# Up-weights' low half in one step, four kinds of side work in half as many visits, and a new list of shifted chunks, in a one-core hybrid decoder layer

## The chip, the cores and the metric

The kernel runs on one core of one Trainium2 chip. The metric is the device time of one launch in microseconds (us). The kernel before takes 1874.46 us in the median of 3 runs (1874.23 to 1876.05).

## What is computed

One decoder layer on 256 tokens of width 2048, in float32. Three sublayers stand behind one another, each with a root-mean-square norm before and after it and a residual:

```python
def hybrid_mixer(h, ...):
    proj = h @ w_in                                    # 2048 x 10536
    mlstm_p, rwkv_p, gate_p = split_cols(proj, ...)
    hm = mlstm_chunkwise(q, k, v, ig, logf)            # 4 heads, key width 128, value width 256
    ha = sigmoid(o) * head_norm(hm)
    rp = rwkv_p + (shift_right(rwkv_p, 1) - rwkv_p) * mu
    w_log = -softplus(-(w0 + tanh(wl) @ w_up)) - 0.5   # w_up: 64 x 1024
    a = sigmoid(a0 + al @ a_up)                        # a_up: 64 x 1024
    g = sigmoid(gl) @ g_up                             # g_up: 160 x 1024
    y = rwkv7_scan(r, decay, kr, v, kk, kk * a)        # 16 heads of 64
    hb = (group_norm(y) + bonus) * g
    merged = sigmoid(g_a) * (ha @ w_branch_a) + sigmoid(g_b) * (hb @ w_branch_b)
    return merged @ w_out

x = x + rms_norm(hybrid_mixer(rms_norm(x)))
x = x + rms_norm(cross_attention(rms_norm(x), rms_norm(mem)))   # 4 heads of 128, 256 memory tokens
x = x + rms_norm(conv_glu_ffn(rms_norm(x)))                     # 2048 -> 2 x 8192 -> 2048, a causal convolution of 3 taps
```

## The kernel before

**The main stream.** All large matrices are cut into 648 pieces of 128 partitions x 1024 elements, called chunks here and numbered in the order in which TensorE (PE) uses them. SyncE loads a chunk's 512 KB into `raw`. ScalarE (ACT) rounds it to `wh` (`Feed.hi`, L376), VectorE (DVE) forms the remainder `wl = raw - wh` (`Feed.lo`, L397). Every product is then the sum of three matmuls, high x high, low x high and high x low. A chunk of a block of kind `fm` gives 24 matmuls with 256 moving columns (128 for each of two `kj` halves times 3), a chunk of kind `tm` 12 matmuls with 512. Each of `raw`, `wh` and `wl` has four buffers, so a cast of chunk i + 4 waits until the matmuls of chunk i are done.

**Blocks and evacuation.** `run` walks through the blocks (16 to 32 chunks of weights that share an accumulator). A finished block leaves a generator (`evac`) that empties its PSUM banks on DVE and ACT. The accumulators are four banks, so a block may begin only when the block two before it has been emptied.

**The side work.** Everything that isn't the main stream, such as gates, group sums, the chunked recurrences and norms, stands in Python generators. `Spread.half` is called at each half chunk (12 `fm` matmuls or 6 `tm` ones) and lets generators go on to their next `yield`, as far as a budget of costs for DVE and ACT allows (`RATE_D`, `RATE_A`, the costs of `Meter`); `side.need` runs a generator to its end at once, where its result is wanted. The order is thus fixed when the program is built, and on the chip each engine works through its list in that order. Where such a generator issues matmuls or transposes, they stand between two main matmuls of PE: the text calls that a visit. "114.12" means behind the 12th main matmul of chunk 114.

The pieces that the change touches, by their names in the profile:

- `uh`, `ul`: high and low half of `up`, the two 64 x 1024 up-projections (`w_up` on partitions 0 to 63, `a_up` on 64 to 127), made in `sm_rest`. The visits `zwa` use them.
- `gcol`, `gbc` (in `gates`): the mLSTM's gate rows, turned into columns and spread over 128 partitions. `gbc` fills one PSUM tile for two heads, and DVE empties it.
- `ssk` (in `k_group`, through `head_sums`): the squared norms of the keys, four groups of two 128-row tiles. Behind each, ACT and DVE form `kt`, `KR` and `BK`.
- `gramA` (in `inverses`): four visits of 16 small matmuls (each counts as two in the profile), each emptied into `comp` by DVE.
- `qk` (in `q_evac`): the queries and keys of the mLSTM leave the accumulators. The first `tm` block behind them (chunk 72) needs those banks.
- `X`, `U`, `Tn`, `Y`, `lv`, `bkt` (in `rwkv`): the chunked recurrence. Ahead of `X`, ACT copies `KR` and the state `T` into `au` in eight steps (`carried`) and the values `vt` in four (`values`).
- `haT` (in `mlstm`): transposes of the mLSTM's output, which ACT and DVE split into `ha`.
- `yT` (in `turned`): transposes of the recurrence's output `ysb`.
- `zg` (in `hb_split`): the output gate, 1024 columns in four steps of 256 and eight matmuls. Two steps share one half of `g_up`, whose parts `gwh` (ACT, three copies, and one DVE subtraction into rows 64 to 95) and `gwl` (DVE) have one buffer each. DVE multiplies the result into `vT`, and ACT and DVE split that into `hb`.
- `xt` (in `x_tokens`): 32 transposes that bring the residual into the layout of the output, in eight visits of four, in the feed-forward sublayer.

**The list of chunks.** `Feed.staged` places a chunk's `wh` and `wl` in a buffer of 1152 elements. The usual place starts at element 16 (0 for `tm` with 512 columns) and sets the two `kj` halves 512 elements apart. For chunks named in `KICK` it differs. Kind 0 starts at 24 and puts the halves 24 elements further apart, kind 1 starts at the usual place with the halves 8 elements further apart.

Of the kernel before, what the change touches and what calls it, by code (L numbers as in the profile page):

```python
# [10 lines left out]
F32R = mybir.dt.float32r  # L11
# [134 lines left out]
def _layer(ctx, tc, nc, d, dbg):  # L146
# [174 lines left out]
    def block(kind, srcs, xs, evac, before=None, cols=512, pool_=None, pre=None, bankwise=False, tail=0):  # L321
# [5 lines left out]
    KICK = {16: 0, 26: 1, 32: 0, 52: 1, 60: 0, 104: 0, 108: 0, 111: 0, 116: 0, 117: 1, 120: 1, 134: 0, 140: 0, 144: 1,  # L327
            159: 1, 168: 0, 215: 0, 218: 1, 235: 0, 242: 0, 256: 0, 280: 1}

    class Feed:  # L330
# [28 lines left out]
        def staged(self, name, r, i):  # L359


            k, c = r.shape[1:]
            kick = KICK.get(i)
            e = -(-c // 64) * 64
            o = 0 if c >= 512 and self.kind[i] == "tm" else 16
            if kick is not None:
                o, e = (24, e + 24) if kick == 0 else (o, e + 8)
            w = wp.tile([P, 1024 + 128], F32R, tag=name, bufs=4, name=name)
            return w[:, o:o + k * e].rearrange("p (k c) -> p k c", k=k)[:, :, 0:c]
# [283 lines left out]
    def sm_rest(wa, gl0, gl1):  # L653
# [3 lines left out]
        for i, h in enumerate(hid):  # L657
            act.copy(h[E2[i]], wa[E2[i]])
            dve.tensor_sub(h[E2[1 - i]], wa[E2[i]], h[E2[i]])
            act.copy(uh[E2[i], i], up[E2[i]])  # L660
            yield
            act.copy(uh[E2[1 - i], i], up[E2[i]])
            dve.tensor_sub(ul[E2[i]], up[E2[i]], uh[E2[i], i])
            yield
# [32 lines left out]
    def gates():  # L697
# [65 lines left out]
        for h2 in range(2):  # L763
            q = aux("gbc", [P, 2, S])
            for j in range(2):
                sel = id4[:, h2 * 2 + j:h2 * 2 + j + 1].broadcast_to((4, P))
                mm(q[:, j], sel, g2[0:4, 0], stop=False)
                mm(q[:, j], sel, g2[0:4, 1], start=False)
            for j in range(2):
# [116 lines left out]
    def inverses():  # L886
# [399 lines left out]
    def hb_split():  # L1286
# [16 lines left out]
        for p2 in range(4):  # L1303
# [9 lines left out]
            s2 = slice(p2 * 2, p2 * 2 + 2)  # L1313
            q = aux("zg", [P, 2, S])
            for j in range(2):
                c = slice(p2 % 2 * 256 + j * P, p2 % 2 * 256 + j * P + P)
                mm(q[:, j], wh[:, 0, c], gs[:, 0], stop=False)
                mm(q[:, j], wh[:, 0, c], gs[:, 1], start=False, stop=False)
                mm(q[:, j], wl[:, c], gs[:, 0], start=False, stop=False)
                mm(q[:, j], wh[0:96, 1, c], g3[0:96], start=False)  # L1320
            for j in range(2):
# [385 lines left out]
    def fu_evac(b):  # L1707
        def gen(ps):
# [86 lines left out]
    def x_tokens():  # L1795

        M["xt"] = []
        for f in range(4):
            if f % 2 == 0:
                M["xt"].append(U("xt", [P, 2, 1024]))  # L1800
            for t in range(2):
                q = aux("xt", [P, 4, P])
                for j in range(4):
                    k = f * 4 + j
                    pe.transpose(q[:, j], M["xr"][k // 8][:, k % 8, t * P:(t + 1) * P], ident)
                act.copy(M["xt"][f // 2][:, t, f % 2 * 512:f % 2 * 512 + 512], q.rearrange("p a b -> p (a b)"))
                yield
# [173 lines left out]
```

## Time and profile before

| | |
|---|---|
| median of 3 runs | 1874.46 us |
| the profiled execution's own time | 1875.39 us |
| its span in the profile | 1873.3 us |
| PE busy | 1862.3 us, 99% |
| DVE busy | 1294.9 us, 69% |
| ACT busy | 1014.5 us, 54% |
| DMA | 351.46 MB, mean 188 GB/s |

The span runs from the first to the last instruction that the profile counts as busy. In the rows of a timeline the columns are the start in us, the busy time in us, the engine, the line, the operation, output<-input with shapes and the count of instructions that the row gathers; in brackets stands the engine's idle time before it and what ended it. Rows of one engine overlap by about a tenth of a microsecond, since an instruction begins before the one ahead has drained. For matmuls the distance from one start to the next tells the pace, not the busy time of one, which is longer.

### The profile page before, as it was taken

To read this page: it belongs to the slowest core of one execution; us is meant where nothing else is said; L and a number is where in the kernel's file an instruction comes from. 1 tells how busy PE (TensorE), PEld (TensorE's weight loads), DVE (VectorE), ACT (ScalarE), POOL (GpSimd) and SP (SyncE) were. 2 spreads that over 40 slices of the span, in tenths; PEclk is the share of its full clock that TensorE was granted. 3 is DMA by queue.
4 is the path that set the end of the run, shared out by engine and by line. 5 is a ranking of instruction groups with operands and counts; after the bars stand their busy time and mean duration, and the time that the engine had idled before them with its cause. 6 is when DMAs were issued, how large, how long until landed. Compare 5 with 4: busy or idle time off the path is not lost.

```text
span 1873.3 us, 36356 instructions
## 1 busy us (share of the span) xinstructions
PE 1862.3 (99%) x15024; PEld 1774.0 (95%) x15024; DVE 1294.9 (69%) x1836; ACT 1014.5 (54%) x1473; POOL 22.3 (1%) x40
## 2 busy tenths in 40 slices
PE   9999999999999999999999999999999999999998
PEld 9999988999999999999999999999999988888887
DVE  7789787666675857687766666777666675556555
ACT  6776435655454645665644455554444555545554
POOL 0000000000000000000000000000000000000000
PEclk9999999999999999999999999999999999999999
DMA  7545544344556765455666666666666666666664
GB/s 260 182 168 202 176 151 159 129 156 156 169 184 202 278 200 185 143 183 171 200 191 196 197 194 192 197 187 195 199 195 196 194 192 214 195 192 197 192 191 145
DMA packets 98197, 351.46 MB, mean 188 GB/s; under 512 B 11056, under 2 KB 11568, under 8 KB 97648
## 3 DMA queue, kind: packets, MB, share of 16 engines
q1 hardware_dynamic: 97168, 348.01, 57.6%
q8 instruction: 117, 1.92, 0.4%
q10 hardware_dynamic: 864, 1.15, 0.2%
q14 instruction: 48, 0.39, 0.1%
HBM read 347.01 MB, written 2.10 MB: 186 GB/s over the span
## 4 chain that ended last, share of the span: by engine, by line
PE 97%; DVE 1%; ACT 1%; DMA 0%; issue 0%; ACTq 0%; DVEq 0%
PE fm L181 67%; PE tm L181 25%; DVE wl L397 1%; PE gram L181 0%; ACT wh L376 0%; PE Y L181 0%; DMA w<-in_w_in_dram 0%; PE num L181 0%; PE lv L181 0%; DVE rows L66 0%; PE X L181 0%; PE gramA L181 0%; PE U L181 0%; PE zg L181 0%; PE zwa L181 0%
## 5 line engine op out<-in xcount | busy, mean ns | idle before, releaser
L397 DVE TENSOR_TENSOR wl<-raw,wh 128x1024 fp32r<-128x1024 f32 (+1 forms) x640 | 775.9, 1217 | 411.7 <-ACT wh L376 407.2
L376 ACT CAST wh<-raw 128x1024 fp32r<-128x1024 f32 (+1 forms) x640 | 664.5, 1043 | 495.9 <-PE fm L181 371.3
L181 PE MATMUL fm<-fh,wh 128*128 128x256 f32 x2048 | 565.9, 277 | 1.4 <-ACT fh L66 1.4
L181 PE MATMUL fm<-fh,wl 128*128 128x256 f32 x2048 | 565.0, 276 | 0.0
L181 PE MATMUL fm<-fl,wh 128*128 128x256 f32 x2048 | 564.9, 276 | 0.0
L181 PEld LDWEIGHTS fm<-fh,wh 128*128 128x128 f32 x2048 | 384.3, 188 | 1.5 <-ACT fh L66 1.5
L181 PEld LDWEIGHTS fm<-fl,wh 128*128 128x128 f32 x2048 | 384.2, 188 | 0.0
L181 PEld LDWEIGHTS fm<-fh,wl 128*128 128x128 f32 x2048 | 384.2, 188 | 0.0
L181 PE MATMUL tm<-wh,as 128*128 128x512 f32 x1024 | 315.4, 389 | 0.0
L181 PE MATMUL fm<-hh,wh 128*128 128x256 f32 x1024 | 284.7, 280 | 1.4 <-ACT wh L387 1.0
L181 PE MATMUL fm<-hh,wl 128*128 128x256 f32 x1024 | 282.3, 278 | 0.8 <-DVE wl L397 0.8
L181 PE MATMUL fm<-hl,wh 128*128 128x256 f32 x1024 | 282.1, 277 | 0.0
L181 PEld LDWEIGHTS tm<-wh,as 128*128 128x128 f32 x1024 | 192.1, 188 | 39.9
L181 PE MATMUL tm<-wl,as 128*128 128x512 f32 x512 | 199.2, 389 | 0.0
L181 PEld LDWEIGHTS fm<-hh,wh 128*128 128x128 f32 x1024 | 191.9, 188 | 3.2 <-ACT wh L387 1.2
L181 PEld LDWEIGHTS fm<-hh,wl 128*128 128x128 f32 x1024 | 191.6, 188 | 1.2 <-DVE wl L397 1.2
L181 PEld LDWEIGHTS fm<-hl,wh 128*128 128x128 f32 x1024 | 191.4, 188 | 0.1
L181 PEld LDWEIGHTS tm<-wl,as 128*128 128x128 f32 x512 | 96.1, 188 | 20.0
L66 ACT CAST as<-ac 128x256 fp32r<-128x256 f32 x128 | 45.6, 404 | 110.8 <-PE tm L181 110.8
L66 DVE TENSOR_TENSOR as<-ac,as 128x256 fp32r<-128x256 f32 x128 | 48.5, 421 | 61.7 <-ACT as L66 61.7
L181 PE MATMUL fm<-mgh,wh 128*128 128x256 f32 x256 | 71.0, 277 | 0.0
L181 PE MATMUL fm<-mgl,wh 128*128 128x256 f32 x256 | 70.8, 277 | 0.0
(384 smaller groups left out, 2217.6 us busy)
## 6 DMA issues: line engine op xcount, KB each, us to landing
raw<-in_w_fu_dram SPq DMA_DIRECT2D x256, 512.0 KB, 4.2
raw<-in_w_in_dram SPq DMA_DIRECT2D x152, 512.0 KB, 3.5
raw<-in_w_fd_dram SPq DMA_DIRECT2D x128, 512.0 KB, 3.8
raw<-in_w_br_dram SPq DMA_DIRECT2D x32, 512.0 KB, 4.0
raw<-in_w_mo_dram SPq DMA_DIRECT2D x32, 512.0 KB, 4.0
raw<-in_w_xk_dram SPq DMA_DIRECT2D x8, 512.0 KB, 3.6
raw<-in_w_xv_dram SPq DMA_DIRECT2D x8, 512.0 KB, 3.7
raw<-in_w_xq_dram SPq DMA_DIRECT2D x8, 512.0 KB, 3.6
```

The costliest lines, as they stand in the source:

```text
L66: return f(out, *a, **k)
L181: pe.matmul(out, lhsT, rhs, start=start, stop=stop, skip_group_check=True)
L376: nc.scalar.copy(wh, r)
L397: nc.vector.tensor_sub(wl, r, self.st[self.nl][0])
```

## The change

- `sm_rest`: the rounded copy `ud` of both up-projections is made in one 128-partition ACT copy at the first of the two turns, and the low half `ul` in one 128-partition DVE subtraction at the second; before, each turn had a 64-partition subtraction.
- `gates`: both `gbc` tiles are filled in one visit of eight matmuls (before two of four).
- `inverses`: the `gramA` matmuls stand in two visits of 32 matmuls with two PSUM tiles each (before four of 16 with one).
- `hb_split`: the `zg` matmuls stand in two visits of 16 (before four steps of 8, the last two of them together in one visit).
- `x_tokens`: four visits of eight transposes, 16 half chunks apart (before eight of four, 8 apart).
- `KICK` is a new list, with a third kind: kind 2 starts at 24 and keeps the halves at the usual distance.

```diff
-    KICK = {16: 0, 26: 1, 32: 0, 52: 1, 60: 0, 104: 0, 108: 0, 111: 0, 116: 0, 117: 1, 120: 1, 134: 0, 140: 0, 144: 1,
-            159: 1, 168: 0, 215: 0, 218: 1, 235: 0, 242: 0, 256: 0, 280: 1}
+    KICK = {16: 0, 31: 0, 52: 2, 60: 1, 104: 1, 107: 1, 110: 1, 114: 1, 137: 0, 140: 0, 143: 0, 147: 1, 162: 1, 168: 0,
+            215: 0, 218: 1, 235: 2, 243: 2, 256: 0, 280: 1}
...
-                o, e = (24, e + 24) if kick == 0 else (o, e + 8)
+                o, e = ((24, e + 24), (o, e + 8), (24, e))[kick]
...
             act.copy(uh[E2[1 - i], i], up[E2[i]])
-            dve.tensor_sub(ul[E2[i]], up[E2[i]], uh[E2[i], i])
+            if i == 0:
+                ud = C("ud", "au1", [P, 1024], F32R)
+                act.copy(ud, up)
+            else:
+                dve.tensor_sub(ul, up, ud)
             yield
...
-        for h2 in range(2):
-            q = aux("gbc", [P, 2, S])
+        qs = [aux("gbc", [P, 2, S]) for _ in range(2)]
+        for h2, q in enumerate(qs):
             for j in range(2):
                 ...
+        for h2, q in enumerate(qs):
             for j in range(2):
...
-            q = aux("gramA", [P, 2, 4, 64])
-            for ci in range(2):
-                for j in range(4):
-                    for e in range(2):
-                        p = hf * 4 + j
-                        mm(q[E2[e], ci, j], KR[E2[e], p, c0 + ci, 0], BK[E2[e], p, c0 + ci, e])
+            if hc % 2 == 0:
+                qs = [aux("gramA", [P, 2, 4, 64]) for _ in range(2)]
+                for c in range(4):
+                    for j in range(4):
+                        for e in range(2):
+                            p = hf * 4 + j
+                            mm(qs[c // 2][E2[e], c % 2, j], KR[E2[e], p, c, 0], BK[E2[e], p, c, e])
+            q = qs[hc % 2]
...
-        for p2 in range(4):
+        for p2 in range(0, 4, 2):
             if p2 % 2 == 0:
                 w = gup[p2 // 2]
                 wh, wl = C("gwh", "bg0", [P, 2, 512], F32R), C("gwl", "bg1", [P, 512], F32R)
...
-            s2 = slice(p2 * 2, p2 * 2 + 2)
-            q = aux("zg", [P, 2, S])
-            for j in range(2):
...
+            qs = [aux("zg", [P, 2, S]) for _ in range(2)]
+            for j in range(4):
+                c = slice(j * P, j * P + P)
+                q = qs[j // 2][:, j % 2]
+                mm(q, wh[:, 0, c], gs[:, 0], stop=False)
+                mm(q, wh[:, 0, c], gs[:, 1], start=False, stop=False)
+                mm(q, wl[:, c], gs[:, 0], start=False, stop=False)
+                mm(q, wh[0:96, 1, c], g3[0:96], start=False)
+            for j in range(4):
                 p = p2 * 2 + j
-                dve.scalar_tensor_tensor(M["bv"][:, p], M["bv"][:, p], pcol("lnb", p), q[:, j], op0=ALU.add, op1=ALU.mult)
-            split(hb[0][:, s2], hb[1][:, s2], M["bv"][:, s2])
-            yield
+                dve.scalar_tensor_tensor(M["bv"][:, p], M["bv"][:, p], pcol("lnb", p), qs[j // 2][:, j % 2],
+                                         op0=ALU.add, op1=ALU.mult)
+                if j % 2:
+                    s2 = slice(p - 1, p + 1)
+                    split(hb[0][:, s2], hb[1][:, s2], M["bv"][:, s2])
+                    yield
...
-                side.add(x_tokens(), chain=8)
+                side.add(x_tokens(), chain=16)
...
+            qs = [aux("xt", [P, 4, P]) for _ in range(2)]
             for t in range(2):
-                q = aux("xt", [P, 4, P])
                 for j in range(4):
                     k = f * 4 + j
-                    pe.transpose(q[:, j], M["xr"][k // 8][:, k % 8, t * P:(t + 1) * P], ident)
-                act.copy(M["xt"][f // 2][:, t, f % 2 * 512:f % 2 * 512 + 512], q.rearrange("p a b -> p (a b)"))
-                yield
+                    pe.transpose(qs[t][:, j], M["xr"][k // 8][:, k % 8, t * P:(t + 1) * P], ident)
+            for t in range(2):
+                act.copy(M["xt"][f // 2][:, t, f % 2 * 512:f % 2 * 512 + 512], qs[t].rearrange("p a b -> p (a b)"))
+            yield
```

Since the order of all side work is fixed by budgets when the program is built, the change also moves instructions that it doesn't name. Visits stand like this, in chunk and main matmul:

| visit | before | changed |
|---|---|---|
| gcol; gbc | 28.12; 30.24 and 31.24 | 28.12; 30.24 |
| ssk, four groups | 42.12, 50.12, 59.12, 65.24 | 42.24, 50.24, 61.12, 67.12 |
| gramA | four, 80.12 to 82.12 | 83.6 and 84.12 |
| second X of the recurrence, and the last haT ahead of it | 114.12, 110.24 | 117.12, 114.12 |
| last X; second yT | 144.12; 159.24 | 147.12; 162.12 |
| zg | 164.12, 164.24, and two at 167.24 | 167.12 and 167.24 |
| xt | eight of four | 281.24, 289.24, 297.24, 305.24 |

The first place is ahead of chunk 72, where the queries leave the accumulators. DVE, from the fourth `ssk` result (`kt<-ssk`) to the first `qk`, before (the row `wl` is the main stream's):

```order
L66 TENSOR_SCALAR kt<-ssk 128x512
L397 TENSOR_TENSOR wl<-raw,wh 128x1024
L66 TENSOR_TENSOR kt<-kt 128x512
...
L66 TENSOR_TENSOR kt<-BK,kt 128x512
L397 TENSOR_TENSOR wl<-raw,wh 128x1024
L66 TENSOR_TENSOR kt<-kt,at 128x512
L397 TENSOR_TENSOR wl<-raw,wh 128x1024
L66 TENSOR_TENSOR BK<-kt 64x8x64 x4
L397 TENSOR_TENSOR wl<-raw,wh 128x1024 x2
L66 SCALAR_TENSOR_TENSOR rr<-rr,par,kt 128x256 x2
L397 TENSOR_TENSOR wl<-raw,wh 128x1024
L66 TENSOR_TENSOR qk<-fm,st_b 128x512 x2
```

and with the change:

```order
L66 TENSOR_SCALAR kt<-ssk 128x512
L397 TENSOR_TENSOR wl<-raw,wh 128x1024
L66 TENSOR_TENSOR kt<-kt 128x512
...
L66 TENSOR_TENSOR kt<-BK,kt 128x512
L397 TENSOR_TENSOR wl<-raw,wh 128x1024
L66 TENSOR_TENSOR kt<-kt,at 128x512
L66 TENSOR_TENSOR BK<-kt 64x8x64 x4
L397 TENSOR_TENSOR wl<-raw,wh 128x1024 x2
L66 SCALAR_TENSOR_TENSOR rr<-rr,par,kt 128x256 x2
L66 TENSOR_TENSOR qk<-fm,st_b 128x512 x2
```

Between the two ends stand six `wl` rows before and four with the change, and on PE 144 and 108 main matmuls between this `ssk` visit and chunk 72. ACT at the same place, with the change: its logarithm and exponential (`kt<-kt`) now have the cast that the first of those `wl` rows reads behind them, where before it stood ahead of them.

```order
L376 CAST wh<-raw 128x1024
L66 ACTIVATE kt<-lw 128x512
L66 ACTIVATE kt<-kt 128x512 x2
L376 CAST wh<-raw 128x1024
L66 ACTIVATE kt<-at,oka,par 128x256 x2
```

The second place is ACT ahead of the second `X` of the recurrence (`au` is its operand, `ha` comes from the transposes `haT` ahead of it), before:

```order
L66 COPY au<-vt 64x256 x4
L66 ACTIVATE ha_4072<-haT,par 128x256 x4
L376 CAST wh<-raw 128x1024 x2
L66 ACTIVATE sg<-sg 128x512
L66 COPY au<-KR 64x256
```

and with the change (`sg` are the branch gates that leave the accumulators):

```order
L66 ACTIVATE sg<-sg 128x512
L376 CAST wh<-raw 128x1024
L66 ACTIVATE sg<-sg 128x512
L66 COPY au<-vt 64x256 x4
L376 CAST wh<-raw 128x1024
L66 ACTIVATE ha_3995<-haT,par 128x256 x4
L376 CAST wh<-raw 128x1024
L66 COPY au<-KR 64x256
```

The values and a second gate stand between the first gate and the splits of `ha` now; the eight copies of `KR` and `T` follow last in both.

The third place is DVE at the output gate. Before, the second half's `gwl` and `gwh` stand behind the work on the first two `zg` results, a chunk's `wl` away, and two more `wl` follow ahead of the last two results:

```order
L66 SCALAR_TENSOR_TENSOR vT<-vT,par,zg 128x256 x2
L66 TENSOR_TENSOR hb_6276<-vT,hb_6275 128x512
L397 TENSOR_TENSOR wl<-raw,wh 128x2x512
L66 TENSOR_TENSOR gwl<-gup,gwh 128x512
L66 TENSOR_TENSOR gwh<-gup,gwh 32x512
L397 TENSOR_TENSOR wl<-raw,wh 128x1024 x2
L66 SCALAR_TENSOR_TENSOR vT<-vT,par,zg 128x256 x2
```

With the change they follow the first visit's work at once, and the second visit stands 12 main matmuls behind the first on PE:

```order
L66 SCALAR_TENSOR_TENSOR vT<-vT,par,zg 128x256 x2
L66 TENSOR_TENSOR hb_6367<-vT,hb_6366 128x512
L66 TENSOR_TENSOR gwl<-gup,gwh 128x512
L66 TENSOR_TENSOR gwh<-gup,gwh 32x512
L66 SCALAR_TENSOR_TENSOR vT<-vT,par,zg 128x256 x2
L66 TENSOR_TENSOR hb_6367<-vT,hb_6366 128x512
L397 TENSOR_TENSOR wl<-raw,wh 128x1024 x4
```

Nothing of the main stream stands between the two halves on DVE now.

More of the change, by code (lines that the diff above doesn't have):

```diff
@@ L1312, in hb_split @@
                     yield
-            s2 = slice(p2 * 2, p2 * 2 + 2)
-            q = aux("zg", [P, 2, S])
-            for j in range(2):
[L1316 to L1321, printed above, removed]
-                p = p2 * 2 + j
-                dve.scalar_tensor_tensor(M["bv"][:, p], M["bv"][:, p], pcol("lnb", p), q[:, j], op0=ALU.add, op1=ALU.mult)
-            split(hb[0][:, s2], hb[1][:, s2], M["bv"][:, s2])
-            yield
+            qs = [aux("zg", [P, 2, S]) for _ in range(2)]
[7 more added lines that the diff above has]
+            for j in range(4):
+                p = p2 * 2 + j
+                dve.scalar_tensor_tensor(M["bv"][:, p], M["bv"][:, p], pcol("lnb", p), qs[j // 2][:, j % 2],
[4 more added lines that the diff above has]
+                    yield
     def gate_evac(i, cb):
```

## The prediction

> **What bounds the kernel now.** I read the page's totals and its chain first, then PE's waits, then the pace of its matmuls by tile and window.
>
> ```profile
> span 1873.3 us, 36356 instructions
> PE 97%; DVE 1%; ACT 1%; DMA 0%; issue 0%; ACTq 0%; DVEq 0%
> PE fm L181 <- ACT fh L66: 1.4, 1, 1.4
> PE fm L181 <- DVE wl L397: 0.8, 1, 0.8
> ```
>
> The chain that ended last is PE's own work; the other engines hold a few per cent of it. The two largest waits inside the stream are 1.4 and 0.8 us. So the time is the number of matmuls times their pace, plus what visits cost beside it, plus waits. A change of side work can win at most the visits' edges and these few waits, and can lose wherever it makes DVE or ACT late for a visit.
>
> The pace has two levels. Each row below gives the busy time of one matmul and the first and last start:
>
> ```profile
> L181 PE MATMUL fm<-hh,wl x45: 281/281/281, 193.9 to 209.5; 128*128 128x256 f32 x45
> L181 PE MATMUL fm<-mgh,wl x109: 276/276/276, 623.2 to 660.0; 128*128 128x256 f32 x109
> L181 PE MATMUL fm<-qh,wh x64: 277/281/283, 740.7 to 763.0; 128*128 128x256 f32 x64
> ```
>
> In the second row 108 steps of three matmuls take 36.8 us, 0.1136 us a matmul; in the first 44 steps take 15.6 us, 0.1182. So a slow chunk of 24 matmuls costs 0.11 us more than a fast one. The first and third rows lie in the two longest slow stretches, chunks 60 to 71 and 235 to 256, worth 1.3 and 2.3 us. By the starts of all main matmuls the slow chunks cost 8.6 us together, and from chunk 266 on all are fast.
>
> **The change, part by part.** *Visits.* A visit's edge is read at `gbc`:
>
> ```profile
> 90.51 0.73 PE L181 MATMUL gbc<-g,id 4*128 4x256 f32 x4
> 91.17 0.39 PE L181 MATMUL fm<-hh,wh 128*128 128x256 f32 x1
> 91.39 0.28 PE L181 MATMUL fm<-hl,wh 128*128 128x256 f32 x1
> ```
>
> From the visit's first matmul to the first main one pass 0.66 us, 0.21 more than four at the fast pace, and the next main start comes 0.22 later instead of 0.11; ahead of the visit it is 0.1 likewise, so the edges cost about 0.4 us. One such visit falls away (0.4), two of `gramA` (their edges between 0.2 and 0.4 each), one of `zg` and four of `xt`, whose transposes run at nearly the main pace (0.03 to 0.04 each). `gcol` becomes a visit of its own (+0.2), `zwa` joins `gbc` and a `lv` joins `den` (-0.2 each). Sum -1.3 (bounds -0.8 and -1.8).
>
> *The low half `ul`.* It counts at one place:
>
> ```profile
> 72.80 0.39 PE L181 MATMUL fm<-hh,wl 128*128 128x256 f32 x1 [0.77 <-DVE wl L397]
> 69.01 1.22 DVE L66 TENSOR_TENSOR ul<-up,uh 64x1024 fp32r<-64x1024 f32 x1
> 73.73 0.91 ACT L66 ACTIVATE rr<-pr,om 128x256 f32<-128x256 f32 x2 [5.45 <-DVE pr L66]
> ```
>
> Ahead of this wait (0.77 on the weight load, 0.93 from matmul start to start over the pace) DVE is busy without a gap and holds two such subtractions of 1.22. A 128-partition one of 1024 elements costs the same as a `wl` row, 1.22, so DVE gains 1.2 and the wait goes: -0.9. The extra ACT copy, about 1.05 like a cast, lies in front of ACT's 5.45 us of idleness. Without that cover the `wl` would come 1.05 later and nothing be won: bounds -0.9 and 0.
>
> *Ahead of chunk 72.* The `ssk` visit moves from 65.24 to 67.12, so 108 main matmuls remain to the first `tm`, which needs the bank that DVE's first `qk` empties. Before:
>
> ```profile
> 192.50 0.28 PE L181 MATMUL ssk<-hsh,bones 128*128 128x256 f32 x1
> 210.24 0.47 PE L181 MATMUL tm<-wh,hh 128*128 128x512 f32 x1
> 193.24 0.69 DVE L66 TENSOR_SCALAR kt<-ssk 128x512 f32<-128x512 f32 x1 [1.18 <-POOL L L894]
> 193.85 1.22 DVE L397 TENSOR_TENSOR wl<-raw,wh 128x1024 fp32r<-128x1024 f32 x1
> 195.30 0.69 DVE L66 TENSOR_TENSOR kt<-kt 128x512 f32<-128x512 f32 x1 [0.23 <-ACT kt L66]
> 208.27 1.23 DVE L397 TENSOR_TENSOR wl<-raw,wh 128x1024 fp32r<-128x1024 f32 x1 [0.81 <-ACT wh L376]
> 209.41 1.28 DVE L66 TENSOR_TENSOR qk<-fm,st_b 128x512 f32<-128x512 f32 x2
> 193.97 1.30 ACT L66 ACTIVATE kt<-kt 128x512 f32<-128x512 f32 x2 [0.34 <-DVE kt L66]
> 196.16 1.03 ACT L376 CAST wh<-raw 128x1024 fp32r<-128x1024 f32 x1
> ```
>
> From `ssk` to the second `kt` it was 2.80. With the change a cast stands behind the two exponentials, and the `wl` that reads it ahead of that `kt`: 0.74 + 0.73 to the exponentials, 1.2 for them, 1.03 for the cast, 1.14 for the `wl`, 4.85. From there to the first `qk`'s end it was 14.75 (209.41 + 0.64 - 195.30). Two `wl` rows fewer take off 2.28, and the idle ahead of the last, 0.81, falls away, since DVE now runs behind the casts: 11.7, or 10.4 if DVE's other small idle goes too. DVE thus needs 15.3 to 16.5. PE needs 0.47 for the visit and 108 times 0.1136 to 0.1182, 12.7 to 13.2. That is a wait of 2.1 to 3.8, against 0.3 before (210.24 stands that much behind the pace). I take +2.4; bounds 0 (the cast comes early) and +3.5.
>
> *The output gate.* Before, the second half's `gwh` and `gwl` were ready ahead of the visit. Now they are written after the first visit has read their only buffers and, in queue order, after the work on its results. The last visit of before, which also holds 16 matmuls, shows what that work takes:
>
> ```profile
> 533.94 0.39 PE L181 MATMUL zg<-gs,gwh 128*128 128x256 f32 x2
> 538.16 0.62 ACT L66 CAST hb<-vT 128x512 fp32r<-128x512 f32 x1 [1.54 <-DVE vT L66]
> 538.82 0.69 DVE L66 TENSOR_TENSOR hb<-vT,hb 128x512 fp32r<-128x512 f32 x1 [0.69 <-ACT hb L66]
> 529.63 1.78 ACT L66 CAST gwh<-gup 128x512 fp32r<-128x512 f32 x3
> 530.90 0.68 DVE L66 TENSOR_TENSOR gwl<-gup,gwh 128x512 fp32r<-128x512 f32 x1
> ```
>
> Counted from the visit's start: ACT's second `hb` ends at 4.84, `gwh` at about 5.4 (a third of 1.78), `gwl` behind DVE's `hb` at 6.2, the rows 64 to 95 of `gwh` at 6.9. PE is back after 1.9 for the visit and 12 main matmuls, at 3.26, and its fourth matmul reads the last of these; three at the pace are 0.34. So the wait is 3.3, in three pieces, the first 2.1. Nothing hides it, since PE has no other work in its queue. Bounds 2.1 and 4.0.
>
> Whether such a stop also costs clock, this stage of before bears on:
>
> ```profile
> 664.00:816.00 152.00, 150.07 (x1259) 148.40 (x1258) 98.13 (x138) 90.50 (x147) 3.09 (x3) 1.00 0.54 173
> ```
>
> Its granted clock is 1.00 with PE's longest stop, 1.4 us, inside. The Trainium skill (TensorE: Matmul & The Clock Gate, "Why this matters for your kernels") says that idle gaps of the array beyond about 3 us between bursts drop it to half clock; no run here shows so long a stop yet. I leave it out of the sum, since the gate's wait comes in pieces of at most 2.1 us, and take it up as a rival.
>
> *The second `X`.* ACT's copies into `au` ended just in time before:
>
> ```profile
> 346.12 1.04 PE L1280 MATMUL haT<-con,so 128*128 128x128 f32 x8
> 356.93 1.15 PE L181 MATMUL X<-au 128*64 128x64 f32 x32
> 345.13 1.65 ACT L66 COPY au<-vt 64x256 f32<-64x256 f32 x4
> 346.81 0.48 ACT L66 ACTIVATE ha<-haT,par 128x256 fp32r<-128x256 f32 x1
> 349.26 0.48 ACT L66 ACTIVATE ha<-haT,par 128x256 fp32r<-128x256 f32 x1 [0.58 <-DVE ha L66]
> 354.24 0.39 ACT L66 COPY au<-KR 64x256 f32<-64x256 f32 x1
> 356.75 0.40 ACT L66 COPY au<-T 64x256 f32<-64x256 f32 x1
> ```
>
> The 10.81 us from `haT` to `X` fall by 12 main matmuls, to 9.45. ACT must now do a gate (0.54, less than half of the pair at 193.97), `vt` 1.65, a cast 0.97, the splits 2.93 (349.26 + 0.48 - 346.81), a cast 0.97 and the copies 2.91, 10.0 us. The gate starts some 1.5 behind `haT` (estimate: a cast, a `wl` and DVE's own product come ahead of it), and a `wl` in front of DVE's share of the splits may add 1.1. The last copy then ends at 11.5 to 12.6 and is read 0.8 into `X`, at 10.25: late by 1.2 to 2.3. I take +1.9; bounds 0.6 and 2.9.
>
> *Smaller ones.* The second `yT` had little room:
>
> ```profile
> 506.94 0.69 DVE L66 TENSOR_TENSOR ysb<-ysb,gr 128x512 f32<-128x512 f32 x1 [0.92 <-POOL gr L226]
> 507.92 1.04 PE L1178 MATMUL yT<-con,ysb 128*128 128x128 f32 x8
> ```
>
> The operand was ready 0.29 us ahead. Two gates of about 0.6 (a row like this one) now stand on DVE between the variances and these products, where one `wl` stood: +0.9 (0 to 1.6). At the last `X` two gates on ACT come ahead of the same eight copies, +0.7 (0 to 1.5); a gate's evacuation at chunk 172 +0.3. The `gramA` results, four emptyings behind one visit instead of one each, are wanted by the 31 steps on DVE only, and PE's next work from them is 15 chunks later: nothing.
>
> *Pace.* The list changes at 60, 137, 143 and 235, where slow stretches began, worth 1.3, 0.4, 0.7 and 2.3, 4.7 in all. At 60 `vt` now meets kind 1 in mid-chunk, as before at 52, where the stretch turned fast after one chunk: -1.3. For the rest (3.4) I take half, -1.7, and +0.6 for visits that now have no shifted chunk behind them (123, 133). Sum -2.4; bounds -6 and +1.5.
>
> **Sum.** -1.3 - 0.9 + 2.4 + 3.3 + 1.9 + 1.9 - 2.4 = +4.9 us; 0.1 off for the pace gained ahead of the wait at 72, which that wait takes back: +4.8. The profiled execution's 1875.39 with span 1873.3 would become 1880.2 and 1878.1; it stands 0.93 above the median. The median 1874.46 becomes 1879.3.
>
> **Rivals.** *The list wins more.* If the shifted places turn all that is slow fast, not a third of it, 7 us come instead of 2.4: +0.2, 1874.7. For it speaks that each slow stretch ends at a visit or a shifted chunk; against it that before's list had a shift at 235 too, and the stretch behind it (the 281 ns row) stayed slow. Without the pace's term the sum is +7.2, so from 3.5 us of cure on the time is within what can be told from no change. *The new waits do not come*, since casts run further ahead than I count: without them -1.3 - 0.9 - 4.7, 1867.6, and the change is faster. Against it stand the single buffers of `gwh`. *The residual's transposes turn the pace slow.* Visits of eight transposes had a shifted chunk behind them before (52, 60, 111, 116); the new `xt` have none, and the next shift after 281 doesn't exist. 238 `fm` chunks from 281 to 518 at 0.11 are 26 us: 1905. Against it: visits of four left the pace fast. *The clock falls behind the gate's stop*: at half pace for as long as PE stood, 3.3 us, it loses half of that, 1.7: 1881.0; against it the pieces, and the clock of 1.00 above. *The moves do nothing*, PE's 97% hide them: then only visits and the low half count, 1872.3, within the measurement.
>
> **How the numbers follow.** What a measurement here can tell from no change is 0.2%, 3.75 us. Forecast (the waits outweigh) 52%, its own range 1876.5 to 1882.5; the list wins more, within 0.2%, 32%; no waits, faster, 8%; slow transposes 5%; the clock 3%. The moves that do nothing are part of the 32%. That is faster 0.08, same 0.32, slower 0.60. The range goes down to 1871.5, where no new wait but the gate's lower bound is left beside the visits, the low half and 2.9 us of pace (-1.3 - 0.9 + 2.1 - 2.9), and up to 1886, the upper ends of the waits without the pace's gain; it leaves out the cases of 8 and 5%.
>
> **What would show it.** A wait of `zg` on ACT's `gwh` of 2 us and on DVE's `gwl` and `gwh`; `tm` on DVE `qk` 2 to 3 us; `X` on ACT `au`; no wait at `wl` near 72 us; 276 ns rows at 194 to 209 and 740 to 763; `xt` followed by 276 ns rows. The forecast is wrong if `zg` and `tm` wait less than 1 us each, or if the 281 ns rows move into the feed-forward stage.

## The result: 2.3% slower

The changed kernel takes 1919.12 us in the median of 4 runs (1913.11 to 1922.94), the kernel before 1875.22 us (1873.3 to 1877.8 in all its runs here); the ratio is 1.0232, with a 95% interval of 1.0221 to 1.0244. The forecast of 1879.3 had the sign and nearly all the new waits, but not the size: 4.8 us were forecast, 43.9 came. The rival of 5%, that visits of eight transposes leave the pace slow, is the larger part of it.

The page of the changed kernel, its totals:

```profile
span 1916.3 us, 36356 instructions
PE 1897.0 (99%) x15024; PEld 1808.6 (94%) x15024; DVE 1295.5 (68%) x1835; ACT 1017.0 (53%) x1472; POOL 22.7 (1%) x40
```

PE does as many matmuls as before (15024 records), is busy for 34.7 us longer, and stands some 8 us more.

PE's waits (engine, tile and line, what it waited for: us in all, times, the longest):

```profile
PE zg L181 <- ACT gwh L66: 3.5, 1, 3.5
PE tm L181 <- DVE qk L66: 2.6, 1, 2.6
PE X L181 <- ACT au L66: 2.1, 4, 0.9
PE yT L1185 <- DVE ysb L66: 0.9, 1, 0.9
PE zg L181 <- DVE gwh L66: 0.4, 1, 0.4
PE zg L181 <- DVE gwl L66: 0.3, 1, 0.3
```

None of these six is in the list of before; each stands at a place that the prediction named. The row of `X` sums two places: three of its pieces, 1.7 us, stand at the second `X`, and one of 0.4 at the last. The wait of 0.8 on `wl` near 72 us is gone. But together they are 9.8 us of 43.

The pace of the matmuls in the feed-forward sublayer, before and with the change (busy time of one in ns: least, median, most):

```profile
L181 PE MATMUL fm<-fh,wl x1758: 276/276/283, 900.0 to 1499.7; 128*128 128x256 f32 x196
```

```profile
L181 PE MATMUL fm<-fh,wl x1837: 280/282/284, 909.8 to 1560.3; 128*128 128x256 f32 x184
```

A whole stage has gone over into the slow pace. In the changed kernel it begins behind the first visit of eight transposes (281.24) and ends with the last `fm` chunk, 519. Between the starts of chunks 276 and 528 the gap to the kernel before grows from 17.7 to 42.9 us: 25.2 us, for 238 chunks 0.106 each. Another such stretch is new, from chunk 172 to 218, where before only 215 to 218 were slow. The rows of the same tile, before and with the change:

```profile
L181 PE MATMUL fm<-hb,wh x192: 276/276/276, 568.6 to 622.8; 128*128 128x256 f32 x192
...
L181 PE MATMUL fm<-hb,wh x192: 280/282/282, 583.5 to 639.8; 128*128 128x256 f32 x192
```

The gap grows by 5.4 us between chunks 168 and 216. Of these, 0.5 are a wait for a gate and 0.4 a stretch of half clock that reaches into chunk 168, so the slow pace costs 4.5. Up to chunk 168 the gap is 13.2 us.

In those 13.2 us lies something that the waits don't show. The table by windows gives busy us (and count) of PE, its weight loads, DVE, ACT and POOL, then the granted clock, the DMA share and GB/s. Around the second `X` with the change:

```profile
360.00:366.00 6.00, 5.19 (x46) 4.95 (x45) 3.53 (x6) 4.10 (x8) 0.00 (x0) 1.00 0.27 87
366.00:370.00 4.00, 3.06 (x42) 2.58 (x44) 1.35 (x2) 3.90 (x9) 0.00 (x0) 0.87 0.39 135
370.00:374.00 4.00, 4.00 (x52) 3.71 (x49) 3.63 (x9) 1.98 (x6) 0.00 (x0) 0.50 0.60 173
374.00:377.00 3.00, 3.00 (x20) 3.00 (x20) 1.93 (x4) 1.04 (x1) 0.00 (x0) 0.70 0.30 119
...
546.00:550.00 4.00, 3.71 (x18) 3.74 (x19) 1.86 (x5) 0.62 (x1) 0.00 (x0) 0.57 0.00 0
```

PE ran at half its clock, for 6.8 us from 368.96 on, late in the `X` visit and behind it, and for 3.4 us from 546.45 on, in the second `zg` visit (last row). Main matmuls start 0.213 us apart there. With them stand the three pieces of the wait at this `X` and, as the last row, the one at the last `X`:

```profile
366.08 0.33 PE L181 MATMUL X<-au 128*64 128x64 f32 x2 [0.89 <-ACT au L66]
366.81 1.07 PE L181 MATMUL X<-au 128*64 128x64 f32 x16 [0.40 <-ACT au L66]
368.27 0.68 PE L181 MATMUL X<-au 128*64 128x64 f32 x14 [0.40 <-ACT au L66]
...
368.88 2.05 PE L181 MATMUL gram<-KR,BK 64*128 64x128 f32 x16
...
372.23 0.41 PE L181 MATMUL fm<-hl,wh 128*128 128x256 f32 x1
372.44 0.42 PE L181 MATMUL fm<-hh,wl 128*128 128x256 f32 x1
...
475.53 0.68 PE L181 MATMUL X<-au 128*64 128x64 f32 x14 [0.40 <-ACT au L66]
```

From the main matmul ahead of the `X` visit to the first one behind it pass 7.16 us instead of 3.23. Told by the starts, 2.7 of the difference lie ahead of 368.88, where the clock was still 1.00: these are the waits, of which the profile counts 1.7 as idle. The other 1.3 are half clock, and 17 main matmuls behind the visit cost 1.7 more. The second `zg` visit takes 8.13 instead of 2.02: 4.9 of waits up to its fourth matmul at 546.29 (4.2 of them idle) and 1.2 of half clock, with 0.4 behind it. So the two falls of the clock cost 4.6 us; the 10.2 us at half clock can cost 5.1 at most.

### The profile page after: what moved, and what is told of

The parts are those of the page before. It is cut to its first block, busy times and chain, and to the rows that moved or that the text cites. A ratio compares the mean times of both kernels' runs of the same rounds, so it can differ in the third digit from the quotient of the medians.

```text
span 1916.3 us, 36356 instructions
## 1 busy us (share of the span) xinstructions
PE 1897.0 (99%) x15024; PEld 1808.6 (94%) x15024; DVE 1295.5 (68%) x1835; ACT 1017.0 (53%) x1472; POOL 22.7 (1%) x40
## 3 DMA queue, kind: packets, MB, share of 16 engines
q10 hardware_dynamic: 864, 1.15, 0.2%
## 4 chain that ended last, share of the span: by engine, by line
PE 86%; ACT 1%; DVE 1%; issue 0%; DMA 0%; SPq 0%; ACTq 0%; DVEq 0%
PE fm L181 58%; PE tm L181 24%; PE gram L181 0%; ACT wh L376 0%; DVE wl L397 0%; ACT au L66 0%; PE Y L181 0%; PE num L181 0%; PE lv L181 0%; DMA gup<-in_g_up_dram 0%; PE U L181 0%; PE gramA L181 0%; PE xsc L181 0%; PE X L181 0%; PE xt L1815 0%
## 5 line engine op out<-in xcount | busy, mean ns | idle before, releaser
L181 PE MATMUL fm<-fh,wh 128*128 128x256 f32 x2048 | 576.0, 282 | 1.4 <-ACT fh L66 1.4
L181 PE MATMUL fm<-fh,wl 128*128 128x256 f32 x2048 | 575.5, 281 | 0.0
L181 PE MATMUL fm<-fl,wh 128*128 128x256 f32 x2048 | 575.5, 281 | 0.0
L181 PEld LDWEIGHTS fm<-fh,wh 128*128 128x128 f32 x2048 | 392.5, 192 | 1.5 <-ACT fh L66 1.5
L181 PE MATMUL fm<-mgh,wl 128*128 128x256 f32 x256 | 71.5, 279 | 0.0
```

The lines of the kernel that those rows point to most:

```text
L181: pe.matmul(out, lhsT, rhs, start=start, stop=stop, skip_group_check=True)
```

## The experiments

Two questions: what makes the pace slow, and whether the merged visits or the order bring the waits. The sentence ahead of each diff says from which kernel it starts.

**Pace: visits of eight against visits of four.** The changed kernel with the `x_tokens` of before (four transposes, one copy, one yield):

```diff
-                side.add(x_tokens(), chain=16)
+                side.add(x_tokens(), chain=8)
...
```

> The changed kernel with the residual's transposes put back to eight visits of four, 8 half chunks apart; all else as changed. Theory P (the eight transposes of a visit at a chunk's end leave PE in its slow pace, and no shifted chunk follows to end it): chunks 282 to 519 run at 113 ns a matmul instead of 118, and the time falls by 24.9 us, what these chunks gained on the kernel before between its chunk 288 and 520, less 0.15 for four more visits: about 1894. Rival L (the new list or an earlier event sets the pace that the feed-forward chunks inherit): they stay at 118 and the time stays at 1919.

Measured: 1895.52 us (1894.68 to 1897.19), ratio to the kernel before 1.0106 (1.0091 to 1.0121). The same tile and window:

```profile
L181 PE MATMUL fm<-fh,wl x1757: 276/276/280, 900.0 to 1499.8; 128*128 128x256 f32 x196
```

23.6 us less, and at the fast pace. The reverse, the kernel before with only these visits changed (eight transposes, then two copies, one yield):

```diff
-                side.add(x_tokens(), chain=8)
+                side.add(x_tokens(), chain=16)
...
```

> The kernel before with only the residual's transposes changed (four visits of eight, 16 half chunks apart). Theory P: chunks 282 to 519 turn slow, +25 us, about 1900. Rival L: the pace there doesn't depend on these visits, 1875.

Measured: 1900.12 us (1899.61 to 1900.38), ratio 1.0129 (1.0112 to 1.0146), 24.5 us more.

```profile
L181 PE MATMUL fm<-fh,wl x1694: 281/281/283, 899.8 to 1499.8; 128*128 128x256 f32 x189
```

The two runs are each other's mirror: the four visits of eight transposes are the cause, with either list of shifted chunks and after either order ahead of them. Neither list has a shifted chunk behind these visits.

**What a shifted chunk does to it.** The changed kernel with four entries more:

```diff
-            215: 0, 218: 1, 235: 2, 243: 2, 256: 0, 280: 1}
+            215: 0, 218: 1, 235: 2, 243: 2, 256: 0, 280: 1, 282: 0, 290: 0, 298: 0, 306: 0}
```

> The changed kernel with its visits of eight transposes, and four entries more in the list of shifted chunks: 282, 290, 298 and 306, of kind 0, each the chunk behind such a visit. Theory P: each shifted chunk costs some 0.1 us and the chunks behind it are fast, about 1894.5. Rival L, and a second rival E (eight transposes in one visit cost by themselves, whatever follows): slow as before, 1919.

Measured: 1891.37 us (1888.62 to 1894.70), ratio 1.0084 (1.0069 to 1.0099). Near the expected time, but not by the expected way. Three windows of this run:

```profile
L181 PE MATMUL fm<-fh,wl x58: 279/281/287, 883.8 to 904.9; 128*128 128x256 f32 x58
...
L181 PE MATMUL fm<-fh,wl x42: 276/276/279, 911.1 to 925.0; 128*128 128x256 f32 x42
...
L181 PE MATMUL fm<-fh,wl x1472: 276/276/276, 999.8 to 1499.9; 128*128 128x256 f32 x184
```

Behind the shift at 282 PE stays slow, behind 290 it is fast, behind 298 slow again (chunks 298 to 306), behind 306 fast to the end. Kind 0 changed the state each time here; that four of them end fast is luck of the count. It is no rule for every visit of eight transposes: in the kernel before, chunks 111 and 134 are of kind 0 and stand behind such visits, and the chunks behind them, 112 and 135, are as fast as those ahead. So two more, from the kernel before with visits of eight. First a single shift, far from any visit:

```diff
-            159: 1, 168: 0, 215: 0, 218: 1, 235: 0, 242: 0, 256: 0, 280: 1}
+            159: 1, 168: 0, 215: 0, 218: 1, 235: 0, 242: 0, 256: 0, 280: 1, 400: 0}
```

> The kernel before with the residual's transposes in four visits of eight, and one more shifted chunk, 400 of kind 0, far behind the last of them and with no visit near. Theory P1 (a shifted chunk by itself ends the slow pace): slow from 282 to 400, fast from 401 to 519, 12.5 us less than without it, 1887.5. Rival P2 (only a visit and a shift together change the pace): slow to 519, 1900.

Measured: 1885.95 us in 2 runs, ratio 1.0061 (1.0041 to 1.0082); 14.2 us below the 1900.12 of the kernel without it, of which 1.0 is the difference of the two chips' kernel before. Its windows ahead of chunk 400 and behind it:

```profile
L181 PE MATMUL fm<-fh,wl x889: 276/281/283, 899.8 to 1214.9; 128*128 128x256 f32 x178
...
L181 PE MATMUL fm<-fh,wl x810: 276/276/276, 1224.7 to 1499.8; 128*128 128x256 f32 x162
```

A shift by itself, with no visit near, ended the slow pace. Then kind 2 (with `Feed.staged` as changed) behind each visit:

```diff
-            159: 1, 168: 0, 215: 0, 218: 1, 235: 0, 242: 0, 256: 0, 280: 1}
+            159: 1, 168: 0, 215: 0, 218: 1, 235: 0, 242: 0, 256: 0, 280: 1, 282: 2, 290: 2, 298: 2, 306: 2}
```

> The kernel before with four visits of eight transposes and a shifted chunk of kind 2 behind each (282, 290, 298, 306). Theory P3 (kind 2 behind a visit of eight leaves the fast pace from either state, as behind the transposes at 51.24 in the changed kernel and at 59.24 in the one with the list set by rows): fast from 283 on, 1875. Rival P4 (it swaps the two states, as kind 0 did): fast and slow by turns from 283 to 306, fast or slow to 519, 1876 to 1900.

Measured: 1874.20 us (1873.66 to 1875.37), ratio 1.0000 (0.9989 to 1.0010). From 282 on only the shifted chunks themselves, 282, 290, 298 and 306, are slow; the row of the tile:

```profile
L181 PE MATMUL fm<-fh,wl x1760: 276/276/287, 899.9 to 1499.9; 128*128 128x256 f32 x196
```

So the harm of the visits of eight is wholly undone by the right kind of shift, and the visits by themselves win nothing that shows: in the traces four visits of eight take 3.64 us of PE with the main matmul beside each, eight of four 3.79, of which four more main matmuls are 0.45. Without these the visits of eight are some 0.3 dearer.

**The stretch from 172.** The changed kernel with visits of four and a shift at 173:

```diff
-            215: 0, 218: 1, 235: 2, 243: 2, 256: 0, 280: 1}
+            215: 0, 218: 1, 235: 2, 243: 2, 256: 0, 280: 1, 173: 2}
```

> The changed kernel with the residual's transposes in visits of four, and one more shifted chunk, 173 of kind 2. It asks for the slow stretch from 172 to 214, which begins at the wait of 0.3 us for a gate. Theory P1: the shift ends it, 4.3 us less than without: 1891.2. Rival P2: it stays, 1895.5.

Measured: 1890.59 us (1886.50 to 1893.70), ratio 1.0079 (1.0062 to 1.0096); without the shift it was 1895.52. But the profiled run is slow through the stretch:

```profile
L181 PE MATMUL fm<-hb,wh x192: 281/281/281, 584.1 to 640.4; 128*128 128x256 f32 x192
```

The rule of P1 fails in that run; whether the shift helped in the others can't be read from their times, which spread over 7 us. What begins this stretch stays open: the kernel with the low half alone, below, has the same wait of 0.3 us at 172 and stays fast there.

**The waits: one edit moves the plan.** The kernel before with only the low half in one step:

```diff
-            dve.tensor_sub(ul[E2[i]], up[E2[i]], uh[E2[i], i])
+            if i == 0:
+                ud = C("ud", "au1", [P, 1024], F32R)
+                act.copy(ud, up)
+            else:
+                dve.tensor_sub(ul, up, ud)
```

> The kernel before with only the low half of the up-weights made in one 128-partition step. Theory S (this edit alone moves the plan of all side work, since the budgets that set the order count its costs, and with the plan come the new waits): waits as in the changed kernel, of the output gate's matmuls on ACT (3.5), of chunk 72 on DVE (2.6), of the second X on ACT (2.1), and the half clock behind two of them, 5 us; with the visits no longer where the list of shifts expects them, some slow stretches on top: 1885 to 1900. Rival M (each merged visit brings the wait behind it; the low half by itself only wins its DVE step): 1874, 0.9 faster.

Measured: 1895.83 us (1893.19 to 1899.49), ratio 1.0108 (1.0093 to 1.0123).

```profile
PE zg L181 <- ACT gwh L66: 3.5, 1, 3.5
PE tm L181 <- DVE qk L66: 3.1, 1, 3.1
PE X L181 <- ACT au L66: 1.9, 4, 0.7
```

Five of the six waits are there, these three, `yT` with 0.8 and `zg` on DVE's `gwh` with 0.2, with `gbc`, `gramA` and `zg` visits not merged. The clock fell to 0.50 in this trace too, for 6.8 us each at chunk 72 and at the gate, and chunks 114 to 134 and 256 to 281 are slow that were mostly fast before. One step of side work, 20 us; together with the 24.5 of the visits of eight alone it comes to nearly the 43.9 of the whole change. The budgets of `Spread` take the cost of each instruction from `Meter`; a copy more on ACT and a subtraction less on DVE at this early place shifted which half chunk every later piece falls into. To test it, the same edit with the copy left uncounted and DVE charged what the old subtraction was:

```diff
-                act.copy(ud, up)
+                nc.scalar.copy(ud, up)
+                dve.spent += 70.0 + 1.04 * 1024
```

> The kernel before with the low half of the up-weights made in one 128-partition step, as in the run that made this edit alone, but with the plan's budgets charged what the two old steps were charged, so that all other instructions keep their order. Theory S (the damage came by the moved plan): none of the new waits, the wait of 0.8 on wl near 72 us gone, 0.9 us faster: 1874.5. Rival (the edit itself makes ACT late, by its cast): the wait at 72 us stays or grows, and no gain, 1875.5 or more.

Measured: 1874.32 us (1873.47 to 1876.05), ratio 0.9995 (0.9986 to 1.0004). None of the waits, and the 0.8 on `wl` is gone from the list too. In its trace the order on PE is that of the kernel before, and the orders on DVE and ACT differ from it in the edit's own instructions alone. 0.9 us faster than the 1875.26 beside it, as expected, though the interval still includes no change. Then the merged visits on top of it, `gates`, `inverses` and `hb_split` as changed, `x_tokens` and the list as before:

```diff
-        for h2 in range(2):
-            q = aux("gbc", [P, 2, S])
+        qs = [aux("gbc", [P, 2, S]) for _ in range(2)]
...
-            q = aux("gramA", [P, 2, 4, 64])
+            if hc % 2 == 0:
+                qs = [aux("gramA", [P, 2, 4, 64]) for _ in range(2)]
...
-        for p2 in range(4):
+        for p2 in range(0, 4, 2):
...
```

> The kernel before with the low half in one step at the old charge, and the merged visits of the inverse grams, the gate rows and the output gate; the residual's transposes in eight visits of four and the list of shifted chunks as before. Theory S: the merged visits bring no wait of their own where the plan stays, the second output gate visit stands far enough behind the first: 0.9 for the low half and about 1.1 for the visits, 1873.5. Rival M (merged visits bring waits): output gate or chunk 72 wait as in the changed kernel, 1879 or more.

Measured: 1872.86 us (1872.01 to 1874.86), ratio 0.9988 (0.9979 to 0.9997). None of the new waits either: `zg` in two visits of 16 costs nothing where the first visit stands at 164.12, three chunks ahead of the second, and not 12 matmuls.

**The list set by the rows.** The kernel that keeps the plan, with kind 2 and this list:

```diff
-    KICK = {16: 0, 26: 1, 32: 0, 52: 1, 60: 0, 104: 0, 108: 0, 111: 0, 116: 0, 117: 1, 120: 1, 134: 0, 140: 0, 144: 1,
-            159: 1, 168: 0, 215: 0, 218: 1, 235: 0, 242: 0, 256: 0, 280: 1}
+    KICK = {16: 0, 32: 0, 52: 1, 60: 2, 104: 0, 108: 0, 111: 0, 116: 0, 117: 1, 120: 1, 134: 0, 137: 0, 140: 0, 145: 0,
+            159: 1, 168: 0, 215: 0, 218: 1, 235: 2, 243: 2, 256: 2, 280: 1}
```

> As the kernel that keeps the plan, with the list of shifted chunks set by the rows of the traces: 60, 235, 243 and 256 of kind 2, 137 and 145 of kind 0 anew, without 26, 144 and 242. Theory P: the slow stretches at 60 to 71, 137 to 139, 145 to 149 and 235 to 249 turn fast, 4 us at most, 1869.5 to 1872. Rival: what a shift does depends on the pace with which PE comes to it, as it did at 282 and 298 with eight transposes (slow) and 290 and 306 (fast), so some stretches change sides: 1873 to 1876.

Measured: 1869.91 us (1868.87 to 1871.90), ratio 0.9970 (0.9958 to 0.9981), faster than both kernels. The two slow stretches that the prediction quoted are fast:

```profile
L181 PE MATMUL fm<-hh,wl x36: 276/276/276, 194.0 to 205.9; 128*128 128x256 f32 x36
...
L181 PE MATMUL fm<-qh,wh x54: 276/276/282, 739.7 to 757.8; 128*128 128x256 f32 x54
```

On top of it the last edit, `x_tokens` as changed, with a shift of kind 2 behind each visit of eight:

```diff
-            159: 1, 168: 0, 215: 0, 218: 1, 235: 2, 243: 2, 256: 2, 280: 1}
+            159: 1, 168: 0, 215: 0, 218: 1, 235: 2, 243: 2, 256: 2, 280: 1, 19: 2, 282: 2, 290: 2, 298: 2, 306: 2}
```

> All five edits of the change, with the plan kept as before by charging the low half what the two old steps were charged, and the list of shifted chunks set by rows: as in the run with the list set by rows, and 19, 282, 290, 298 and 306 of kind 2 more. Theory: no wait that the kernel before hasn't, fast from 283 on, 1869.9 less 0.15 for four visits and less some 0.4 where 19 ends a slow start: 1869.4. Rival: one of the shifts swaps fast for slow, 1870 to 1895.

Measured: 1870.84 us (1869.67 to 1872.00), ratio 0.9975 (0.9966 to 0.9984), beside a kernel before of 1875.62 on that chip. That is above the 1869.4 expected, and the last edit brings nothing that shows; the expectation left out that the four shifted chunks are slow themselves (0.1 us each). Of the six new waits its list holds one:

```profile
PE tm L181 <- DVE qk L66: 0.3, 1, 0.3
```

So the edits, with a list made for the order as it is, are worth 4.8 us here, and 5.4 without the last edit. By the steps between the medians these 5.4 are 0.9 for the low half, 1.5 for the merged visits and 3.0 for the list, the first two of them small beside the spread of the runs. What cost 43 us was where the plan put the side work, and shifts that were missing.

**The clock.** The kernel before with ACT's eight copies ahead of the second `X` made twice:

```diff
-                    act.copy(ab[hf][E2[e], e], KR[E2[e], hf * 4:hf * 4 + 4, c, 0])
-                    act.copy(uv[hf][E2[e], e], T[hf][E2[e]])
+                    for again in range(2 if c == 1 else 1):
+                        copy = nc.scalar.copy if again else act.copy
+                        copy(ab[hf][E2[e], e], KR[E2[e], hf * 4:hf * 4 + 4, c, 0])
+                        copy(uv[hf][E2[e], e], T[hf][E2[e]])
```

> The kernel before with ACT's eight copies ahead of the second X made twice, without charge to the plan: nothing else moves, X waits some 2.3 us in two pieces. Theory C (waits of some 2 us spread over a visit of small matmuls are enough to halve the clock for about 3.4 to 7 us behind it): granted clock 0.50 there, about 2.3 + 3.5, 1881. Rival (the half clock in the changed kernel has another cause): clock 1.00, the wait alone, 1878.

Measured: 1877.34 us in the median of 10 runs (1876.70 to 1879.76), ratio 1.0013 (1.0003 to 1.0022). The runs stand in two groups, six from 1876.70 to 1877.42 and four from 1878.57 to 1879.76. The profiled run, of the second group by its span of 1877.7, waits 1.7 us and loses its clock:

```profile
PE X L181 <- ACT au L1034: 1.7, 2, 1.0
```

```profile
356.00:360.00 4.00, 2.33 (x37) 1.94 (x38) 0.29 (x1) 3.95 (x10) 0.00 (x0) 0.88 0.01 4
360.00:364.00 4.00, 4.00 (x54) 3.71 (x52) 3.44 (x7) 2.17 (x6) 0.00 (x0) 0.50 0.49 146
```

The kernel before has 1.00 in these windows:

```profile
356.00:360.00 4.00, 4.00 (x91) 3.60 (x91) 1.76 (x2) 3.90 (x9) 0.00 (x0) 1.00 0.14 51
360.00:364.00 4.00, 4.00 (x37) 4.00 (x37) 3.91 (x10) 1.90 (x4) 0.00 (x0) 1.00 0.76 260
```

So such waits are enough, as theory C says, but not in every execution. The mean granted clock that is on record for each run divides them in the same way: 0.999 to 1.000 in the six, 0.997 to 0.998 in the four. The changed kernel's spread, 1913 to 1923, has in part the same origin: from its fastest run to its slowest the mean clock goes from 0.998 to 0.995, which over 1917 us is some 6 of the 10 us (an estimate from these two figures).

## Why the prediction was wrong

- **What bounds the kernel** held: PE's pace, visits and waits, with its clock, make up the whole difference.
- **The visits** (-1.3) came to about -1, inside their bounds. The `gramA` visits went from 5.61 to 4.67 us over four and two visits, less two main matmuls of 0.23 each that were counted with them, -0.5; the `gbc` group -0.3; the edges behind the four visits that fell away there and at `zg` -0.1 each, and the `xt` visits +0.3.
- **The low half at 72 us** (-0.9) held: the wait, 0.93 from start to start, is gone in the changed kernel and in the run of that edit at the old charge.
- **Ahead of chunk 72** (+2.4) held. From 0.43 to 2.87 us between two starts, +2.4, by the mechanism named: the `wl` waits for the cast behind the two exponentials.

```profile
197.99 1.23 DVE L397 TENSOR_TENSOR wl<-raw,wh 128x1024 fp32r<-128x1024 f32 x1 [2.30 <-ACT wh L376]
199.13 0.69 DVE L66 TENSOR_TENSOR kt<-kt 128x512 f32<-128x512 f32 x1
210.05 0.47 PE L181 MATMUL tm<-wh,hh 128*128 128x512 f32 x1 [2.58 <-DVE qk L66]
```

- **The output gate** (+3.3) had the right chain and was 1.6 short: 4.9 from start to start. I counted DVE's first product 1.15 behind the visit's start, as in the row of before; here two `wl` rows that stand ahead of it in DVE's order came late and it began 2.67 behind 537.76, which makes 1.5 of the 1.6.

```profile
538.15 2.36 DVE L397 TENSOR_TENSOR wl<-raw,wh 128x1024 fp32r<-128x1024 f32 x2 [0.84 <-ACT wh L376]
540.43 0.86 DVE L66 SCALAR_TENSOR_TENSOR vT<-vT,par,zg 128x256 f32<-128x256 f32 x2
544.01 1.78 ACT L66 CAST gwh<-gup 128x512 fp32r<-128x512 f32 x3
544.68 0.51 PE L181 MATMUL zg<-gs,gwh 128*128 128x256 f32 x2 [3.47 <-ACT gwh L66]
```

- **The second X** (+1.9) held within its bounds of 0.6 and 2.9: 2.7 from start to start. The smaller ones came to 1.3, 1.1 and 0.5 instead of 0.9, 0.7 and 0.3.
- **The clock** was the first step that failed. I left it out of the sum because the gate's wait comes in pieces of at most 2.1 us, and gave 3% to a fall there. The first piece was 3.5 us, and the fall there cost 1.6, near the 1.7 of the rival. And I looked for a stop in one piece: at `X` the clock fell with none longer than 0.9, and the 3.0 us of that fall stood in no term and no rival. Together 4.6 us.
- **The pace** was the step that made the prediction wrong. The sum gave it -2.4, and nothing for the visits of eight without a shifted chunk, which stood as a rival of 5%, priced at 26 us. The rival happened, at 25.2. I had written down what spoke for it, that the visits of eight in the kernel before had a shifted chunk behind them (so it is at 59.24, 110.24, 115.24 and 133.24; at 52 the visit stands inside the shifted chunk), and gave more weight to visits of four leaving the pace fast, which the run with visits of eight alone shows to be no argument: the two differ in just this. The stretch from 172, 4.5 us, was not forecast, and its cause is open. Of the cures, 236 to 241 and 244 to 250 are fast with the change, but 256 to 263 and 151 to 153 have turned slow, and 60 to 71 are slow as before. That the slow chunks outside the two new stretches still cost 1.9 us less, near the -2.4, is partly luck: 0.7 of it are chunks 1 to 7, fast in this execution and slow in the profiled one of before, and slow again in that of the changed kernel with visits of four.
- The rival that the moves do nothing and the one that the list wins more were wrong for this kernel. That the list can win shows only with the plan kept: 3.0 us between the two medians of the kernels with and without it.

The sum with the measured terms, from start to start: 2.4 + 4.9 + 2.7 + 2.9 of waits, 4.6 of clock, 25.2 + 4.5 of pace in the two new stretches and -1.9 outside them, -0.9 at 72 us and about -1 for the visits are 43.4; the spans differ by 43.0.

## What to carry to other kernels

Where a planner sets the order from the cost of each instruction, an edit of one small step is an edit of the whole order: read the new order at every visit with little slack, and charge the plan the old cost if only the step is meant (20 us here for a step worth 0.9). A pace that has two levels is a state, not a cost: ask of each edit what ends the slow state behind it, and price it over the whole stretch up to the next thing that can end it. A fall of the clock is to be counted as a chance, with its price, wherever PE's stops add up to some 1.4 us or more within 3.4 us, in one piece or in several; here it came in some executions and not in others.

## What the hardware showed that I had not expected

- Eight transposes of 128 x 128 between two chunks turned the stream of matmuls from 0.113 to 0.118 us each; four did not. The state then held for 238 chunks, to the last `fm` chunk, or until a chunk came by whose weight columns start 24 elements into the buffer (chunk 400 in the run with the single shift). A shift of kind 0 behind the eight `xt` transposes changed the state in either direction; kind 2 led to the fast one each of the eight times that it stood there, but at 173 it changed nothing in the profiled run. What makes the two paces is not shown by any run here.
- The same stop costs clock in one execution and not in another. Behind PE's single stop of 2.6 us at chunk 72 the granted clock stayed at 1.00 in the trace of the changed kernel (first two rows) and fell to 0.50 for 3.4 us in that of the changed kernel with visits of four, which has the same stop (last row):

```profile
207.00:211.00 4.00, 1.42 (x8) 1.10 (x8) 4.00 (x7) 1.04 (x1) 0.00 (x0) 1.00 0.58 183
211.00:215.00 4.00, 4.00 (x19) 3.29 (x19) 1.70 (x2) 1.05 (x1) 0.00 (x0) 1.00 0.57 214
...
210.00:214.00 4.00, 3.12 (x8) 2.52 (x9) 2.46 (x4) 0.00 (x0) 0.00 (x0) 0.57 0.74 250
```

The traces show what decides. Away from the kernel's start and end, six of them hold 13 falls, at chunk 72, at the second `X` or at the gate, each of 3.41 or 6.83 us. Within a trace all falls and recoveries lie whole multiples of 3.413 us apart: in the changed kernel's, 368.96 and 546.45 are 52 of them apart. Laid out from these points, each of the eight windows of 3.41 us in which PE stood for 2.05 us or more ends in a fall, and none with less than 1.39 does; in between it goes either way. The stop at chunk 72 was cut into 1.1 and 1.5 us by such a grid line in the changed kernel's trace, and lay with 2.2 us in one window in the other. The three falls at the second `X` in kernels with its wait of three pieces, and the one with doubled copies, came behind windows with 1.4 to 1.75 us; that the small matmuls there count for little is a guess.

The Trainium skill (TensorE: Matmul & The Clock Gate, "What's actually happening") describes a free-running window of about 3.4 us after which an idle array drops to half clock. The traces agree with the window's length and with its running freely; but here windows were enough in which PE stood for 1.4 to 3.2 of the 3.41 us. So the rule that the prediction took from the same page, no gap beyond about 3 us, is not enough by these traces.
